# Interleaving the 128-column blocks of the up, down, output and gate weight tiles

## The chip, the core and the metric

The kernel runs on one core of a Trainium2 chip. The core has five engines with queues of their own: TensorE (PE in the rows, with its weight loads listed apart as PEld), VectorE (DVE), ScalarE (ACT), GpSimd (POOL) and SyncE (SP), which here issues the DMAs. The metric is the device time of one execution in microseconds (us), the median of several runs. The rows come from one profiled execution.

## What is computed

Two layers of a hybrid transformer block on 512 tokens with 1024 features, in float32. Cut to the lines whose weights the change touches (`w_out`, `w_ffn_up`, `w_ffn_down`, `w_ple_gate`):

```
merged = jnp.einsum('bsnd,nbsd->bsd', gates, branch)
x = x + rms_norm(merged @ w_out, g_post_mix)

h2 = rms_norm(x, g_pre_ffn)
f = jnp.square(jax.nn.relu(h2 @ w_ffn_up)) @ w_ffn_down
x = x + rms_norm(f, g_post_ffn)

ple = (p_i.astype(x.dtype) @ w_ple) * jax.nn.sigmoid(x @ w_ple_gate)
return x + rms_norm(ple, g_post_ple)
```

Ahead of these lines each layer has a wide input projection, a sparse attention, a linear recurrence, a spatial gate and a branch projection; their weights stay as they are.

## The kernel before

Activations lie transposed: features on the 128 partitions, the 512 tokens along the free dimension, so that a product of 1024 features is eight blocks of 128. A weight tile is a matrix of 128 partitions by 1024 floats, and for the four matrices of the change it holds the eight 128x128 blocks that make one output tile of 128 features: block k stands at columns 128k to 128k+127.

Weights come through one pipeline, in the order of the list `order`. `prep` (L230 and after) lets SyncE fetch a tile into `wr` (L236), rounds it on ScalarE into `wh` (L242), and lets VectorE subtract for the remainder `wl` (L243). `getw` hands the pair out and prepares up to three tiles ahead; four pairs of buffers turn.

A product in near-float32 precision is three matmuls in fp32r per block: `wh` with the high part of the activations, `wl` with the high part, `wh` with the low part (`mm3`, L296 to L299). The weight block is the stationary operand (128 columns, loaded by an LDWEIGHTS ahead of each matmul, the PEld rows), the activations are the moving one. `gemm` (L301) runs the eight blocks one after the other, so that a tile is 24 weight loads and 24 matmuls.

Which way a tile takes decides how many tokens move per load:

- `gemm` with all 512 tokens: all 32 down tiles of a layer, 28 of its 32 up tiles, five of eight output tiles, one of eight gate tiles.
- `gemm_halves` (L324 and after): the last three output tiles and the last three gate tiles, first for tokens 0 to 255, then for 256 to 511, so that the norm of the first half starts while the second is multiplied. A tile is then 48 loads and 48 matmuls of 256 tokens. It calls `gemm`, so its rows too bear L297 to L299.
- `gemm_arriving` (L337 and after, matmul at L355): several output tiles at once, block by block as the normed activations arrive. The first four up tiles go this way in halves of 256 tokens, the first four gate tiles with 512.

The input projection (95 of 303 tiles), the branches and the token-wise projections use the same pipeline and the same matmul helpers. The order in which the instructions stand on each engine is written by the program; a running count of estimated time (`tick`) places deferred tasks of the attention, and it doesn't look at the weights' layout.

`_pack` lays the weights out on the host, outside the measured time. In `tiles` the block index k is the slower column index.

Of the kernel before, what the change touches and what calls it, by code (L numbers as in the profile page):

```python
# [19 lines left out]
KT = 8  # L20
# [15 lines left out]
    + [f"g{n}_{d}" for n in range(3) for d in range(8)]  # L36
)
TILE_AT = {n: i for i, n in enumerate(TILES)}


V_PRE, V_POST, V_FFN, V_PFFN, V_PPLE = 0, 8, 16, 24, 32
# [9 lines left out]
def hybrid_block_kernel(ctx, tc, xT, pT, pos, vec, bsp, freq, w_in, w_tok, w_lru, w_sp, w_br, w_out, w_up, w_dn, w_ple, w_gate, out, depth=DEPTH, dbg=None):  # L51
    nc = tc.nc
    V, A, G, PE = nc.vector, nc.scalar, nc.gpsimd, nc.tensor
# [9 lines left out]
    def nm(p):  # L63
        uid[0] += 1
        return f"{p}_{uid[0]}"
# [7 lines left out]
    def bank():  # L73
        return pp.tile([128, 512], F32, tag="ps", name=nm("ps"), bufs=8)
# [8 lines left out]
    def width(r):  # L83
        return r.stop - r.start
# [82 lines left out]
    for l in range(depth):  # L167
        def t_in(n, l=l):
            order.append((("in", l, n), w_in[l, TILE_AT[n]]))

# [55 lines left out]
    prepared = {}  # L226
    LA = NWB - 1
# [18 lines left out]
    def getw(key, ahead=LA):  # L246
        assert order[nget[0]][0] == key, (order[nget[0]][0], key)
        nget[0] += 1
        while nprep[0] < min(nget[0] + ahead, len(order)):
            prep()  # L250
        return prepared.pop(key)

# [30 lines left out]
    def tick(us):  # L285
        clk[0] += us
        run_later()
        run_tasks()
# [4 lines left out]
            tick(0.3)  # L293


    def mm3(ps, wh, wl, xh, xl, start, stop):  # L296
        PE.matmul(ps, wh, xh, start=start, stop=False)  # L297
        PE.matmul(ps, wl, xh, start=False, stop=False)  # L298
        PE.matmul(ps, wh, xl, start=False, stop=stop)  # L299

    def gemm(ps, w, xs, kk, c0=0, st=None, r=FULL):  # L301

        h3, l3 = [v.rearrange("p (k c) -> p k c", k=kk) for v in w]
        for k in range(kk):
            if st is not None and k == kk - 2:
                st.partial()
            mm3(ps, h3[:, k, c0:c0 + 128], l3[:, k, c0:c0 + 128], xs[k][0][:, r], xs[k][1][:, r], k == 0, k == kk - 1)
            tick(0.65 * width(r) / S)

    @contextmanager  # L310
# [23 lines left out]
    def gemm_arriving(keys, xs, source, ranges, arrived=None, lag=LAG, tail=TAIL):  # L334


        n = len(keys)  # L337
        ws = [getw(key, 0) for key in keys[:-1]]
        pss = [bank() for _ in keys]
        last = {}  # L340
        for r in ranges:
            gen = source(r)
            for k in range(KT):
                with ordered(last):
                    next(gen)
                    todo = [(o, k) for o in range(len(ws))]
                    if len(ws) < n and k == lag:
                        ws.append(getw(keys[-1], 0))
                        todo += [(n - 1, q) for q in range(k + 1)]
                    if r is ranges[-1] and k >= KT - tail:  # L350
                        todo = [] if k < KT - 1 else [(o, q) for o in range(n) for q in range(KT - tail, KT)]
                    for i, (o, q) in enumerate(todo):
                        h3, l3 = [v.rearrange("p (k c) -> p k c", k=KT) for v in ws[o]]
                        for m in range(3):
                            PE.matmul(pss[o][:, r], (h3, l3, h3)[m][:, q], xs[q][m // 2][:, r], start=q == 0 and m == 0, stop=q == KT - 1 and m == 2)  # L355
                        if r is ranges[-1] and q == KT - 1 and o < n - 1:
                            prep()
                tick(0.65 * len(todo) * width(r) / S)
            if arrived is not None:
                arrived(r)  # L360
        while nprep[0] < nget[0] + LA:
            prep()
        return pss
# [84 lines left out]
    class Norm:  # L448
# [16 lines left out]
        def source(self, r):  # L465
            while r.start not in self.gens:
                tick(0.1)
            return self.gens[r.start]
# [41 lines left out]
    for key, src in order[:3]:  # L510
        raw = wp.tile([128, 1024], F32, tag="wr", name=nm("wr"), bufs=3)
        hi = wp.tile([128, 1024], F32R, tag="wh", name=nm("wh"), bufs=NWB)
        lo = wp.tile([128, 1024], F32R, tag="wl", name=nm("wl"), bufs=NWB)
# [3 lines left out]
    for k in range(KT):  # L517
        if k in FIRST:
            c = slice(128 * k, 128 * (FIRST + [KT])[FIRST.index(k) + 1])
# [12 lines left out]
    for l in range(depth):  # L532
# [45 lines left out]
        def tokens(n, fn):  # L578


            ws = [[v.rearrange("p (k c) -> p k c", k=2) for v in getw(("tok", l, n, c), LA if c == 0 else 0)] for c in range(4)]
            for t0 in (0, 2):
                pss = [bank(), bank()]
                for k in range(KT):
                    wh, wl = [v[:, k % 2] for v in ws[k // 2]]
                    for t, ps in enumerate(pss, t0):
                        xh, xl = [v[:, t * 128:(t + 1) * 128] for v in XS[k]]
                        for i, (x, w) in enumerate(((xh, wh), (xl, wh), (xh, wl))):
                            PE.matmul(ps, x, w, start=k == 0 and i == 0, stop=k == KT - 1 and i == 2)  # L589
                        tick(0.65)  # L590
                    if t0 == 2 and k in (1, 3, 5):
                        prep()
                for t, ps in enumerate(pss, t0):
                    fn(t, ps)
# [7 lines left out]
        for j in range(4):  # L602
            ps = first[j]
# [13 lines left out]
        ps = proj("ki")  # L617
# [28 lines left out]
        for j in range(4):  # L646
            ps = proj(f"qi{j}")
# [103 lines left out]
        for j in range(4):  # L751
            ps = proj(f"zu{j}")
# [1 line left out]
            V.tensor_mul(zz, ps, R)  # L754
            A.activation(gzu[:, j], zz, AF.Gelu_apprx_tanh)
        run_later(force=True)
        wsh, wsl = [w.rearrange("p (j c) -> p j c", j=4) for w in getw(("sp", l))]
        GG = []

        def gelu_gate(j, ahead=LA):  # L760
# [8 lines left out]
        for j in range(4):  # L769
# [3 lines left out]
            for hf in range(2):  # L773
                ps = bank()
# [4 lines left out]
                for s in range(2):  # L779
                    r = slice(64 * s, 64 * s + 64)  # L780
# [50 lines left out]

        for j in range(2, 4):
            gelu_gate(j)
        w3 = [w.rearrange("p (k c) -> p k c", k=8) for w in getw(("lru", l))]
        Rg = []
        for j in range(4):
            if j == 2:
# [6 lines left out]
            r, i = tmp(), tmp()  # L844
# [165 lines left out]
        for j in range(4):  # L1010
            f = rope(proj(f"q{j}"))
            q2, ql = (slot(f"A{j}", F32R), slot(f"A{4 + j}", F32R)), tmp(F32R)
            for s in range(2):
                r, other = slice(64 * s, 64 * s + 64), slice(64 - 64 * s, 128 - 64 * s)
# [15 lines left out]
        for d in range(8):  # L1030
            if d % 2 == 0:
                w = getw(("br", l, 0, d // 2))
            branch(0, d, w, YA, TH[d])
            hi, lo = mh[d // 4][:, d % 4], ml[d // 4][:, d % 4]
# [12 lines left out]
        for d in range(5):  # L1047
            ps = bank()
# [8 lines left out]
        ps = bank()  # L1057
# [52 lines left out]
        for c in range(2):  # L1110
            w = getw(("ple", l, c), ahead=1)
            if c == 1:
                bc = st3.rstd_bc()
            for i in range(4):
                ps = bank()
# [14 lines left out]
        for d in range(5):  # L1130
            if d < 4:
                ps = first[d]
            else:
                ps = bank()
# [29 lines left out]
def _pack(inputs):  # L1164
    import numpy as np

    def c(a):
        return np.ascontiguousarray(a)

    n = {k: np.asarray(v) for k, v in inputs.items()}  # L1170
    L = DEPTH
    r = {}
    r["xT"] = c(n["x"][0].T).reshape(8, 128, S)
    r["pT"] = c(n["p"][:, 0].transpose(0, 2, 1).reshape(L, 2, 128, S).transpose(0, 2, 1, 3))
    r["pos"] = c(n["positions"].reshape(4, 128).T)

    def cols(a):
        return a.reshape(L, -1, 128).transpose(0, 2, 1)

    r["vec"] = c(np.concatenate(  # L1180
        [cols(n[k]) for k in ("g_pre_mix", "g_post_mix", "g_pre_ffn", "g_post_ffn", "g_post_ple", "conv_w", "conv_b", "b_rg_a", "b_rg_x", "lru_lambda", "g_gmlp_v")],
        axis=2))
    r["bsp"] = c(n["b_spatial"].reshape(L, 4, 2, 128).transpose(0, 2, 1, 3).reshape(L, 2, 512))
    r["freq"] = _freq()

    def tiles(w, nk):

        m = w.shape[2] // 128
        return c(w.reshape(L, nk, 128, m, 128).transpose(0, 3, 2, 1, 4).reshape(L, m, 128, nk * 128))

    w = n["w_in"]
    q, k, v, qi, ki, wi, rest = np.split(w, np.cumsum([512, 512, 512, 512, 64, 8]).tolist(), axis=2)
    pad = np.zeros((L, D, 56), w.dtype)
    xr_zu, zv, g = np.split(rest, [1536, 2048], axis=2)
    r["w_in"] = tiles(np.concatenate([ki, wi, pad, qi, q, k, xr_zu, g], axis=2), 8)
    r["w_tok"] = c(np.stack([v, zv], 1).reshape(L, 2, 4, 2, 128, 512).transpose(0, 1, 2, 4, 3, 5).reshape(L, 2, 4, 128, 1024))
    lru = np.zeros((L, 128, 8, 128), w.dtype)
    for i, key in enumerate(("w_rg_a", "w_rg_x")):
        for b in range(8):
            o = 64 * (b % 2)  # L1200
            lru[:, o:o + 64, 4 * i + b // 2, o:o + 64] = n[key][:, b]
    r["w_lru"] = lru.reshape(L, 128, 1024)
    r["w_sp"] = c(n["w_spatial"].transpose(0, 3, 1, 2).reshape(L, 128, 1024))
    r["w_br"] = c(n["w_branch"].reshape(L, 3, 4, 128, 4, 256).transpose(0, 1, 4, 3, 2, 5).reshape(L, 3, 4, 128, 1024))
    r["w_out"] = tiles(n["w_out"], 8)
    r["w_up"] = tiles(n["w_ffn_up"], 8)
    r["w_dn"] = c(n["w_ffn_down"].reshape(L, 4, 8, 128, 8, 128).transpose(0, 1, 4, 3, 2, 5).reshape(L, 4, 8, 128, 1024))
    r["w_ple"] = c(n["w_ple"].reshape(L, 2, 128, 2, 512).transpose(0, 3, 2, 1, 4).reshape(L, 2, 128, 1024))
    r["w_gate"] = tiles(n["w_ple_gate"], 8)
    return r  # L1210


# [17 lines left out]
```

## Time and profile before

| | us |
|---|---|
| median of 3 runs (lowest, highest) | 1858.88 (1858.13, 1859.21) |
| profiled execution, whole | 1859.11 |
| its span, first to last instruction | 1857.4 |
| TensorE matmul busy | 1804.0 (97%) |
| TensorE weight load busy | 1507.9 (81%) |
| VectorE busy | 1161.0 (63%) |
| ScalarE busy | 800.9 (43%) |
| GpSimd busy | 361.3 (19%) |

TensorE has 8798 matmuls and as many weight loads in the record. A matmul's busy time in a row includes the time in which its last columns travel through the array, and so rows of successive matmuls overlap; what one costs in a stream is the distance between two starts. The same holds for the loads: a row's duration is longer than what a load takes from the next one. PEclk, the clock that TensorE was granted, is 1.00 (2.4 GHz) in nearly the whole span, and 0.50 (1.2 GHz) in a few short stretches.

### The profile page before, as it was taken

How to read it: one execution, taken by the hardware profiler on the slowest of the kernel's cores; microseconds unless marked ns; L12 is line 12 of the kernel's file. 1: busy time of each engine (PE TensorE's matmuls, PEld its weight loads, DVE VectorE, ACT ScalarE, POOL GpSimd, SP SyncE). 2: the span in 40 equal slices, each digit the busy share in tenths (PEclk: the TensorE clock that was granted, in tenths of full speed). 3: DMA queues.
4: the chain of work that ended last, by engine and by line, in shares of the span. 5: the costliest groups of instructions: out<-in, count | busy, mean ns of one | idle time of the engine just before them, and what ended most of it. 6: DMA issues, size and time to landing. Idle time of an engine off the chain costs nothing.

```text
span 1857.4 us, 22874 instructions
## 1 busy us (share of the span) xinstructions
PE 1804.0 (97%) x8798; PEld 1507.9 (81%) x8798; DVE 1161.0 (63%) x1939; ACT 800.9 (43%) x1292; POOL 361.3 (19%) x292
## 2 busy tenths in 40 slices
PE   8899999999999999999998999999999999999997
PEld 7787777888888888888887877877888888888886
DVE  6689986666386253533685999866563852545355
ACT  5466435564353231323554572455544432222233
POOL 3513212210140000003354141222003200000033
PEclk9999999999999999999999999999999999999998
DMA  5122222222223222232212122221222222222321
GB/s 172 63 91 90 87 97 84 76 78 82 80 91 103 100 93 102 91 114 91 89 60 97 66 93 92 102 80 69 91 80 91 91 91 102 92 101 94 111 80 58
DMA packets 49678, 167.77 MB, mean 90 GB/s; under 512 B 6048, under 2 KB 8864, under 8 KB 49568
## 3 DMA queue, kind: packets, MB, share of 16 engines
q1 hardware_dynamic: 47376, 163.64, 25.7%
q10 hardware_dynamic: 2192, 2.67, 0.4%
q8 instruction: 69, 1.13, 0.2%
q14 instruction: 41, 0.34, 0.1%
HBM read 164.19 MB, written 2.10 MB: 90 GB/s over the span
## 4 chain that ended last, share of the span: by engine, by line
PE 72%; DVE 14%; POOL 5%; issue 4%; ACT 4%; DMA 0%; SPq 0%; POOLq 0%; DVEq 0%; ACTq 0%
PE ps L297 20%; PE ps L299 20%; PE ps L298 20%; PE ps L589 4%; PE ps L355 4%; DVE wl L243 2%; DVE tmp L706 2%; DVE m L704 2%; POOL tmp L574 1%; POOL tmp L575 1%; PE ps L958 1%; POOL sacc L397 1%; POOL X L482 1%; PE ps L671 1%; DVE tmp L781 1%
## 5 line engine op out<-in xcount | busy, mean ns | idle before, releaser
L242 ACT CAST wh<-wr 128x1024 fp32r<-128x1024 f32 x303 | 316.7, 1049 | 453.2 <-PE ps L299 369.2
L243 DVE TENSOR_TENSOR wl<-wr,wh 128x1024 fp32r<-128x1024 f32 x303 | 386.0, 1278 | 190.7 <-ACT wh L242 189.9
L297 PE MATMUL ps<-xh,wh 128*128 128x512 f32 (+1 forms) x1296 | 502.2, 388 | 0.0
L298 PE MATMUL ps<-xh,wl 128*128 128x512 f32 (+1 forms) x1296 | 495.1, 382 | 3.0 <-DVE wl L243 3.0
L299 PE MATMUL ps<-xl,wh 128*128 128x512 f32 (+1 forms) x1296 | 495.4, 382 | 0.0
L397 POOL TENSOR_TENSOR sacc<-sacc,tmp 128x256 f32<-128x256 f32 (+1 forms) x99 | 109.7, 1109 | 893.7 <-issue 584.5
L299 PEld LDWEIGHTS ps<-xl,wh 128*128 128x128 f32 x1296 | 243.7, 188 | 48.2
L298 PEld LDWEIGHTS ps<-xh,wl 128*128 128x128 f32 x1296 | 244.0, 188 | 46.9 <-DVE wl L243 3.8
L297 PEld LDWEIGHTS ps<-xh,wh 128*128 128x128 f32 x1296 | 243.8, 188 | 45.5 <-issue 1.9
L299 PE MATMUL ps<-V,wh 128*128 128x512 f32 (+1 forms) x528 | 195.5, 370 | 0.0
L297 PE MATMUL ps<-K,wh 128*128 128x512 f32 (+1 forms) x432 | 158.2, 366 | 0.0
L298 PE MATMUL ps<-K,wl 128*128 128x512 f32 (+1 forms) x432 | 157.9, 365 | 0.0
L299 PE MATMUL ps<-B,wh 128*128 128x512 f32 x336 | 131.0, 390 | 0.0
L297 PE MATMUL ps<-A,wh 128*128 128x512 f32 x320 | 125.0, 391 | 0.0
L298 PE MATMUL ps<-A,wl 128*128 128x512 f32 x320 | 124.6, 389 | 0.0
L1089 DVE TENSOR_TENSOR M<-M,ps 128x512 f32<-128x512 f32 x48 | 33.0, 688 | 141.4 <-PE ps L299 141.4
L299 PEld LDWEIGHTS ps<-V,wh 128*128 128x128 f32 x528 | 99.5, 188 | 16.8
L1077 DVE TENSOR_TENSOR tmp<-ps,R 128x512 f32<-128x512 f32 x64 | 43.9, 691 | 108.4 <-PE ps L299 108.4
L355 PE MATMUL ps<-xl,wh 128*128 128x256 f32 (+1 forms) x264 | 88.2, 334 | 7.7 <-DVE xl L502 6.9
L297 PEld LDWEIGHTS ps<-K,wh 128*128 128x128 f32 x432 | 81.5, 189 | 13.2
L298 PEld LDWEIGHTS ps<-K,wl 128*128 128x128 f32 x432 | 81.5, 189 | 13.1
L355 PE MATMUL ps<-xh,wh 128*128 128x256 f32 (+1 forms) x264 | 86.5, 328 | 1.0 <-ACT xh L492 1.0
(237 smaller groups left out, 2738.5 us busy)
## 6 DMA issues: line engine op xcount, KB each, us to landing
wr<-in_w_in_dram SPq DMA_DIRECT2D x95, 512.0 KB, 3.2
wr<-in_w_up_dram SPq DMA_DIRECT2D x64, 512.0 KB, 3.2
wr<-in_w_dn_dram SPq DMA_DIRECT2D x64, 512.0 KB, 3.2
wr<-in_w_br_dram SPq DMA_DIRECT2D x24, 512.0 KB, 3.2
wr<-in_w_tok_dram SPq DMA_DIRECT2D x16, 512.0 KB, 3.2
wr<-in_w_out_dram SPq DMA_DIRECT2D x16, 512.0 KB, 3.2
wr<-in_w_gate_dram SPq DMA_DIRECT2D x16, 512.0 KB, 3.2
X<-in_xT_dram SPq DMA_DIRECT2D x8, 256.0 KB, 5.2
```

The costliest lines, as they stand in the source:

```text
L242: A.copy(hi, raw)
L243: V.tensor_sub(lo, raw, f32v(hi))
L297: PE.matmul(ps, wh, xh, start=start, stop=False)
L298: PE.matmul(ps, wl, xh, start=False, stop=False)
L299: PE.matmul(ps, wh, xl, start=False, stop=stop)
L355: PE.matmul(pss[o][:, r], (h3, l3, h3)[m][:, q], xs[q][m // 2][:, r], start=q == 0 and m == 0, stop=q == KT - 1 and m == 2)
L397: G.tensor_add(sacc[:, r], sacc[:, r], self.q[r.start, r.stop])
L589: PE.matmul(ps, x, w, start=k == 0 and i == 0, stop=k == KT - 1 and i == 2)
L704: V.max(m8, (sc if r == 0 else wk)[:, :n])
L706: V.match_replace(wk[:, :n], m8, (sc if r == 0 else wk)[:, :n], -3.0e38)
L1077: V.tensor_mul(t, ps, R)
L1089: V.tensor_add(F[d], F[d], ps)
```

## The change

The eight blocks of a tile are laid into each other column by column. With a step of n, n neighbouring blocks form a group, and column c of the group's blocks stand side by side: column c of block k lies at position (k // n) * 128n + c * n + k % n of the tile. The step is 8 for the down and output tiles, 4 for the up tiles and 2 for the gate tiles. A stationary block is then read as 128 floats at a distance of 8, 4 or 2 floats (32, 16 or 8 bytes) where they were neighbours. `_pack` does the laying out; `getw` returns a third value, a function that gives the view of block k; the callers that need the plain pair take the first two. On every engine the same instructions stand in the same order with the same waits; the DMAs, ScalarE's rounding and VectorE's subtraction work on whole tiles as before. Only the access pattern of the stationary operand differs.

```
+STEP = {"up": 4, "dn": 8, "gate": 2, "out": 8}
...
-        return prepared.pop(key)
+        hi, lo = prepared.pop(key)
+        return hi, lo, lambda kk: blocks(key, (hi, lo), kk)
...
+    def blocks(key, w, kk):
+
+
+        n = STEP.get(key[0])
+        if n is None:
+            b = [v.rearrange("p (k c) -> p k c", k=kk) for v in w]
+            return lambda m, k, c0=0: b[m][:, k, c0:c0 + 128]
+        b = [v.rearrange("p (a c b) -> p a b c", b=n, c=128) for v in w]
+        return lambda m, k, c0=0: b[m][:, k // n, k % n]
...
-        h3, l3 = [v.rearrange("p (k c) -> p k c", k=kk) for v in w]
+        b = w[2](kk)
...
-            mm3(ps, h3[:, k, c0:c0 + 128], l3[:, k, c0:c0 + 128], xs[k][0][:, r], xs[k][1][:, r], k == 0, k == kk - 1)
+            mm3(ps, b(0, k, c0), b(1, k, c0), xs[k][0][:, r], xs[k][1][:, r], k == 0, k == kk - 1)
...
+    def mixed(key, a):
+
+        return c(a.reshape(a.shape[:-1] + (8 // STEP[key], STEP[key], 128)).swapaxes(-2, -1).reshape(a.shape))
...
-    r["w_out"] = tiles(n["w_out"], 8)
-    r["w_up"] = tiles(n["w_ffn_up"], 8)
+    r["w_out"] = mixed("out", tiles(n["w_out"], 8))
+    r["w_up"] = mixed("up", tiles(n["w_ffn_up"], 8))
...
-    r["w_gate"] = tiles(n["w_ple_gate"], 8)
+    r["w_gate"] = mixed("gate", tiles(n["w_ple_gate"], 8))
```

`gemm_arriving` takes its blocks from the same function, and `w_dn` is wrapped in `mixed("dn", ...)` in the same way.

## Rows read from the trace of the kernel before

**Rows 1.** The page's first part: busy us (share of the span) and instructions.

```profile
PE 1804.0 (97%) x8798; PEld 1507.9 (81%) x8798; DVE 1161.0 (63%) x1939; ACT 800.9 (43%) x1292; POOL 361.3 (19%) x292
```

**Rows 2.** Busy time by stretch: up and down products of layers 0 and 1.

```profile
core 0: us, PE busy (x) PEld busy (x) DVE busy (x) ACT busy (x) POOL busy (x), PEclk, DMA share, GB/s
546.80:866.30 319.50, 319.50 (x1413) 264.63 (x1412) 149.37 (x180) 90.81 (x108) 10.42 (x6) 1.00 0.29 99
1463.70:1783.10 319.40, 319.40 (x1411) 264.51 (x1410) 149.28 (x179) 90.81 (x108) 10.43 (x6) 1.00 0.29 99
```

**Rows 3.** Timeline, a down product: start us, duration us, engine, line, operation.

```profile
699.68 0.39 PE L299 MATMUL ps<-B,wh 128*128 128x512 f32 x1
...
701.04 0.39 PE L299 MATMUL ps<-B,wh 128*128 128x512 f32 x1
...
699.91 0.19 PEld L298 LDWEIGHTS ps<-A,wl 128*128 128x128 f32 x1
700.14 0.19 PEld L299 LDWEIGHTS ps<-B,wh 128*128 128x128 f32 x1
```

**Rows 4.** Timeline, loads with two moving columns each (sums for the norm).

```profile
866.51 0.63 PEld L407 LDWEIGHTS ps<-ones,sacc 128*128 128x128 f32 x5
```

**Rows 5.** Timeline, output tiles in halves of 256 tokens.

```profile
496.73 0.28 PE L297 MATMUL ps<-K,wh 128*128 128x256 f32 x1
...
498.53 0.28 PE L297 MATMUL ps<-K,wh 128*128 128x256 f32 x1
```

**Rows 6.** Busy time by stretch: output halves, the first up tiles, both layers.

```profile
495.30:513.10 17.80, 17.80 (x151) 17.80 (x150) 4.77 (x7) 8.44 (x17) 6.49 (x8) 1.00 0.21 74
513.20:540.60 27.40, 25.80 (x206) 24.65 (x205) 22.76 (x45) 16.53 (x37) 19.31 (x23) 1.00 0.12 39
1430.00:1457.40 27.40, 25.81 (x205) 24.68 (x205) 22.75 (x45) 16.46 (x37) 19.34 (x23) 1.00 0.12 40
```

**Rows 7.** Waits of TensorE from 495.3 to 546 us: total, times, longest.

```profile
PE ps L355 <- DVE xl L502: 1.0, 2, 0.7
PE ps L433 <- POOL rt L427: 0.4, 1, 0.4
```

**Rows 8.** Timelines and their granted clock (PEclk): 256 and 512 tokens at 0.50.

```profile
931.80:934.00 2.20, 2.20 (x12) 2.20 (x12) 1.92 (x6) 1.24 (x4) 2.18 (x3) 0.50 0.16 65
...
932.00 0.41 PE L355 MATMUL ps<-xh,wl 128*128 128x256 f32 x1
...
933.28 0.41 PE L355 MATMUL ps<-xh,wl 128*128 128x256 f32 x1
...
1000.28 0.63 PE L589 MATMUL ps<-wh,xl 128*128 128x512 f32 x1
...
1001.99 0.63 PE L589 MATMUL ps<-wl,xh 128*128 128x512 f32 x1
```

**Rows 9.** Timeline and granted clock of the warm-up: bf16, 64 moving columns.

```profile
6.20:7.00 0.80, 0.80 (x34) 0.80 (x31) 0.49 (x1) 0.80 (x3) 0.00 (x0) 1.00 1.14 100
...
6.12 0.92 PEld L113 LDWEIGHTS <-bias 128*128 128x128 bf16 x29
```

More of the change, by code (lines that the diff above doesn't have):

```diff
@@ L352, in gemm_arriving @@
                     for i, (o, q) in enumerate(todo):
-                        h3, l3 = [v.rearrange("p (k c) -> p k c", k=KT) for v in ws[o]]
+                        b = ws[o][2](KT)
                         for m in range(3):
-                            PE.matmul(pss[o][:, r], (h3, l3, h3)[m][:, q], xs[q][m // 2][:, r], start=q == 0 and m == 0, stop=q == KT - 1 and m == 2)
+                            PE.matmul(pss[o][:, r], b((0, 1, 0)[m], q), xs[q][m // 2][:, r], start=q == 0 and m == 0, stop=q == KT - 1 and m == 2)
                         if r is ranges[-1] and q == KT - 1 and o < n - 1:
@@ L578, in tokens @@
         def tokens(n, fn):
-            ws = [[v.rearrange("p (k c) -> p k c", k=2) for v in getw(("tok", l, n, c), LA if c == 0 else 0)] for c in range(4)]
+            ws = [[v.rearrange("p (k c) -> p k c", k=2) for v in getw(("tok", l, n, c), LA if c == 0 else 0)[:2]] for c in range(4)]
             for t0 in (0, 2):
@@ L756, in hybrid_block_kernel @@
         run_later(force=True)
-        wsh, wsl = [w.rearrange("p (j c) -> p j c", j=4) for w in getw(("sp", l))]
+        wsh, wsl = [w.rearrange("p (j c) -> p j c", j=4) for w in getw(("sp", l))[:2]]
         GG = []
@@ L833, in hybrid_block_kernel @@
             gelu_gate(j)
-        w3 = [w.rearrange("p (k c) -> p k c", k=8) for w in getw(("lru", l))]
+        w3 = [w.rearrange("p (k c) -> p k c", k=8) for w in getw(("lru", l))[:2]]
         Rg = []
@@ L1204, in _pack @@
     r["w_br"] = c(n["w_branch"].reshape(L, 3, 4, 128, 4, 256).transpose(0, 1, 4, 3, 2, 5).reshape(L, 3, 4, 128, 1024))
-    r["w_out"] = tiles(n["w_out"], 8)
-    r["w_up"] = tiles(n["w_ffn_up"], 8)
-    r["w_dn"] = c(n["w_ffn_down"].reshape(L, 4, 8, 128, 8, 128).transpose(0, 1, 4, 3, 2, 5).reshape(L, 4, 8, 128, 1024))
+    r["w_out"] = mixed("out", tiles(n["w_out"], 8))
+    r["w_up"] = mixed("up", tiles(n["w_ffn_up"], 8))
+    r["w_dn"] = mixed("dn", c(n["w_ffn_down"].reshape(L, 4, 8, 128, 8, 128).transpose(0, 1, 4, 3, 2, 5).reshape(L, 4, 8, 128, 1024)))
     r["w_ple"] = c(n["w_ple"].reshape(L, 2, 128, 2, 512).transpose(0, 3, 2, 1, 4).reshape(L, 2, 128, 1024))
-    r["w_gate"] = tiles(n["w_ple_gate"], 8)
+    r["w_gate"] = mixed("gate", tiles(n["w_ple_gate"], 8))
     return r
```

## The prediction

> **What bounds the kernel now.** I read the shares first: matmuls are busy in 97% of the span, weight loads in 81%, no other engine in more than 63% [rows 1]. Then I looked at the largest stretch that the change touches, the up and down products: in 319.5 us of each layer TensorE has no idle time at the full clock, while VectorE is busy for 149 us and ScalarE for 91 [rows 2]. So these stages cost what the stream of loads and matmuls on TensorE costs, and nothing that another engine gains or loses is seen.
>
> Next, the distance between starts. In the timeline of a down product six matmuls of 512 tokens take 701.04 - 699.68 = 1.36 us, 0.227 each [rows 3]. The load of each following matmul starts as its predecessor starts, so the two run side by side, and the question is how much of the 0.227 a load needs. Its duration of 0.19 us contains latency. The products with `ones` show it better: there only two columns move per load, and five loads lie within 0.63 us, the last with the 0.19 of the loads in [rows 3]: (0.63 - 0.19) / 4 = 0.110 us from load to load [rows 4]; with times rounded to 0.01 us that is 0.108 to 0.113, and I use 0.111. Beside a matmul of 512 tokens a load thus has 0.227 - 0.111 = 0.116 us to spare: it could double and still just fit (0.222 against 0.227).
>
> With 256 tokens it is another matter. In the output halves 15 matmuls take 498.53 - 496.73 = 1.80 us, 0.120 each [rows 5], against a load of 0.111: the load has 0.009 to spare, and a slower one is on the path at once.
>
> **The change part by part.** It moves, adds and removes no instruction. DMAs, rounding and subtraction treat the whole tile, and the extra views are made while the program is built: these edits cost nothing, with no cover needed. What is left is 128 stationary columns read at a distance of 8, 4 or 2 floats. The affected matmuls, both layers together:
>
> - 512 tokens, step 8 or 4: down 64 tiles x 24 = 1536; up 56 x 24 = 1344; output 10 x 24 = 240. Together 3120.
> - 256 tokens, step 8 or 4: output 6 x 48 = 288; the first four up tiles 8 x 48 = 384. Together 672.
> - Step 2: gate, 240 of 512 tokens and 288 of 256.
>
> No row of this kernel shows a load at a distance. The lower bound is a load that doesn't change (x1), and a load that disturbs the stream less lies below nothing; that is a rival. For the upper bound I take the only loads here that are read in another way, the bf16 loads of the warm-up: 29 loads of 128 columns in 0.92 us, at most 0.032 each at the same clock [rows 9], against 0.111. The same number of columns can thus differ by 3.5 according to how they are read, and I let a load at a distance cost up to four times as much (0.444). Between x1 and x4 no row is nearer to one end; I take their middle in ratio, x2 = 0.222 us, for the steps 4 and 8, and x1 for the step 2, which still finds every second float of what it passes.
>
> The Trainium skill, page "SBUF — State Buffer", section "Specifications (TRN2)", speaks against the change: a line has 16 bytes, and two hits per line are needed for full bandwidth. By it the step 2 (two floats to a line) is free, and 4 and 8 (one to a line) pay alike. It gives no size, and no run so far shows it; the split between steps above would be the same by it, and steps priced evenly would add the gate's 288 short matmuls, 29 us.
>
> The terms, with loads of 0.222:
>
> 1. *512 tokens.* 0.222 still fits into 0.227, so the least is 0. But load and stream side by side do cost something at the full clock: at half clock 256 tokens take (933.28 - 932.00) / 6 = 0.213 [rows 8], half of which is 0.107; load 0.111 and stream 0.107 together take 0.120 [rows 5], 0.009 over the longer. So 0 to 0.009 per matmul. At half clock, where both are slower, 0.213 is just what 256 columns take at 1.2 GHz, nothing added, which speaks for 0. I take the middle, 0.004: 3120 x 0.004 = 12.5 us (0 to 28).
> 2. *Output halves.* From 0.120 to 0.222: 288 x 0.102 = 29.4 us. Nothing covers it, since TensorE is busy throughout the stretch [rows 6].
> 3. *First up tiles.* A stretch of 27.4 us for 192 matmuls per layer [rows 6]. The matmuls take 192 x 0.120 = 23.0, norm sums and turns about 1.3 (eight loads of 0.111 and four like them), and 3.1 are idle or paced by arriving activations; TensorE's named waits are 1.0 for `xl` and 0.4 for the norm's factor [rows 7]. With 0.222 the matmuls take 42.6 and arrivals no longer pace them, but the named waits remain: 42.6 + 1.3 + 1.4 = 45.3. That is 17.9 us more per layer, 35.8 for both (33 to 39).
> 4. *Gate.* Step 2 at x1: 0.
>
> Sum: 12.5 + 29.4 + 35.8 + 0 = 77.7 us. Later VectorE and ScalarE have more time, so nothing else becomes late: beside slower matmuls their work is hidden as before. The profiled execution took 1859.11 us, 0.2 above the median of 1858.88, so 77.7 over either gives **1937 us**, 4.2% slower. With loads of 1.5 times (0.167) the halves alone cost 672 x 0.047 = 32 us; with a little more than x2, where the 512-token term reaches 0.013 each, the sum is 41 + 65 + some 7. The case's own range is 1890 to 1975.
>
> **The rivals.**
>
> *The load keeps its pace.* If one float per read is all that a load ever takes, a distance costs nothing: 1859 us. For it: at half clock the load slows with the array (TensorE's 256-token distance doubles to 0.213 and no load sticks out [rows 8]), so the array, not the reading, may set the 0.111. Against it: the bf16 loads are 3.5 times as fast [rows 9].
>
> *Loads at a distance disturb the stream, or take four times as long.* At full clock a matmul of 512 tokens takes 0.227, while half of the half-clock distance, (1001.99 - 1000.28) / 4 / 2, is 0.214 [rows 8]; with 256 tokens it is 0.120 against 0.107. Both exceed by 0.013, whatever the length, so this is a price per load and matmul pair. If it is the load's reading that holds up the moving operand's, and four places have to be read where one was, it is 0.053: 0.040 more for 3792 matmuls and 0.013 for the gate's 528 make 152 + 7 = 159 us, and up to 195 with the doubled load on the halves: 2018 to 2053. With loads of 0.444 the 512-token matmuls are bound by them too: 3120 x 0.217 + 672 x 0.324 = 895 us, some 2750. It decides as soon as a load exceeds 0.227. The Trainium skill, same page, section "Who interferes with whom", speaks against the first form: TensorE's moving operand and its weight load have independent read ports. No row tells whose the 0.013 is.
>
> *Reading at a distance disturbs less* (ends on the other side). If the 0.013 comes from neighbouring floats of the load meeting the stream's reading in the same place, spreading them may remove it: at most 3120 x 0.0135 = 42 us, 1817; half of it 1838. For it: the excess is there only at full clock. Against it: it is equal for all moving tensors in [rows 3, 5], which lie at different places.
>
> **How the numbers follow.** Load about twice as long, 43%: 1890 to 1975, likeliest 1937. Pace kept, 24%: 1859. Stream disturbed 12% (2018 to 2053) or four times as long 6% (some 2750). Disturbs less, 15%: 1817 to 1855. The range 1836 to 2040 leaves out the four-fold case, the top of the disturbed one and the lower half of the faster one, some 17 in 100 together. A measurement of this kernel can tell 0.2% (3.7 us) from no change. Faster 0.15, within 0.2% 0.24, slower 0.61.
>
> **What would show it.** In the profile after: the distance of the 256-token starts in the output halves (0.222, or 0.120 if the pace is kept) and of the first up tiles; the distance in a down product (0.227 to 0.236); the weight loads' mean duration, 0.30 at steps 4 and 8 against 0.19 at the gate and the input projection, which is not touched. The forecast is wrong if steps 4 and 8 differ, if step 2 pays, or if the down products lengthen by more than the halves do.

## The result and the profile after

The changed kernel took 1976.5 us (median of four runs, 1973.7 to 1977.1), the kernel before 1858.5 on the same chip: a ratio of 1.0632, 95% interval 1.0614 to 1.0651. The change costs 118 us. The forecast was 1937, in a range of 1836 to 2040: right in direction and mechanism, 40 us short in size, and 1.5 us beyond the 1975 at which the forecast's own case ended. The profiled execution after took 1976.1 us, of which the span is 1974.4, against 1857.4 for the span before.

The first part of the page after, to be laid beside [rows 1]:

```profile
PE 1923.6 (97%) x8798; PEld 1751.0 (89%) x8798; DVE 1159.6 (59%) x1939; ACT 801.3 (41%) x1292; POOL 362.9 (18%) x292
```

The same instructions ran. Weight loads are busy 243 us longer, matmuls 120 us, and every other engine as long as before; so the new time is on TensorE alone. Its time without work hardly changed: 53.4 us of the span before (1857.4 - 1804.0), 50.8 after.

Next the stretches. The columns are those of [rows 2]; the rows are most of the up and down products of layer 0 (1392 matmuls), one block of eight up tiles (192 matmuls), one of eight down tiles (192), the output halves with what stands beside them, the first up tiles, and a piece of the gate with 512 tokens.

```profile
core 0: us, PE busy (x) PEld busy (x) DVE busy (x) ACT busy (x) POOL busy (x), PEclk, DMA share, GB/s
585.00:918.50 333.50, 333.50 (x1392) 333.42 (x1392) 147.38 (x177) 88.94 (x106) 8.63 (x5) 1.00 0.29 94
694.50:739.60 45.10, 45.10 (x193) 45.10 (x193) 23.15 (x29) 13.24 (x16) 0.00 (x0) 1.00 0.29 94
739.70:786.50 46.80, 46.80 (x193) 46.80 (x193) 16.51 (x18) 9.03 (x9) 0.00 (x0) 1.00 0.27 90
497.40:532.70 35.30, 35.30 (x152) 35.30 (x151) 7.28 (x12) 9.05 (x18) 7.31 (x8) 1.00 0.15 48
532.80:578.70 45.90, 45.90 (x205) 45.90 (x204) 20.84 (x40) 16.50 (x36) 18.48 (x22) 1.00 0.09 26
939.00:961.30 22.30, 22.30 (x97) 18.47 (x96) 16.01 (x20) 11.25 (x18) 5.68 (x5) 1.00 0.16 53
```

In the first row the loads are busy in all 333.5 us, where before they had gaps (264.63 of 319.50 in [rows 2]). That fits stages that now wait for their loads, but load rows overlap one another (the output halves were full of them before, 17.80 of 17.80 us in [rows 6]), so it does not prove it. Per matmul an up tile (step 4) costs 45.1 / 192 = 0.235 us, a down tile (step 8) 46.8 / 192 = 0.244, a gate tile (step 2) 22.3 / 96 = 0.232, where all of them stood at 0.227 before [rows 3]. The first up tiles went from 27.4 [rows 6] to 45.9 us, and the 1.4 us of named waits there [rows 7] are gone: TensorE is busy throughout.

The timeline of the output halves (start us, duration us, engine, line, operation), to be laid beside [rows 5]; between the two rows lie six more starts:

```profile
499.80 0.41 PE L312 MATMUL ps<-K,wl 128*128 128x256 f32 x1
...
501.48 0.40 PE L313 MATMUL ps<-V,wh 128*128 128x256 f32 x1
```

1.68 us for seven distances is 0.240, where it was 0.120. The weight loads of five stretches, grouped (busy us, mean ns of one | idle before them): up tiles, down tiles, output halves, gate with 512 tokens, gate halves:

```profile
L311 PEld LDWEIGHTS ps<-xh,wh 128*128 128x128 f32 x64 | 19.8, 310 | 0.0
...
L313 PEld LDWEIGHTS ps<-B,wh 128*128 128x128 f32 x64 | 21.1, 329 | 0.0
...
L313 PEld LDWEIGHTS ps<-V,wh 128*128 128x128 f32 x20 | 6.8, 338 | 0.0
...
L369 PEld LDWEIGHTS ps<-xh,wl 128*128 128x128 f32 x32 | 6.2, 193 | 1.3
...
L313 PEld LDWEIGHTS ps<-xl,wh 128*128 128x128 f32 x28 | 5.5, 195 | 0.0
```

At steps 4 and 8 a load lasts 0.31 to 0.34 us, at step 2 0.19, as all did before. These durations are 0.08 to 0.1 us longer than the distance from load to load (before: 0.19 against the 0.111 of [rows 4]), so they alone do not give the pace of the loads; the experiments do.

**Where the 118 us lie.** The distance between starts, averaged over all matmuls of a kind in both layers, before and after, times their number:

| matmuls | step | before us | after us | number | difference us |
|---|---|---|---|---|---|
| down, 512 tokens | 8 | 0.2268 | 0.2445 | 1536 | 27.2 |
| up, 512 tokens | 4 | 0.2271 | 0.2358 | 1344 | 11.7 |
| output, 512 tokens | 8 | 0.2267 | 0.2446 | 240 | 4.3 |
| gate, 512 tokens | 2 | 0.2267 | 0.2333 | 240 | 1.6 |
| output halves | 8 | 0.1209 | 0.2412 | 288 | 34.6 |
| first up tiles (stretches of 27.4 and 45.9 us) | 4 | | | 2 x 192 | 37.0 |
| gate halves | 2 | 0.1209 | 0.1212 | 288 | 0.1 |

Together 116.5, which is all but 1.5 us of the difference. The tiles of the input projection, which were not touched, kept their mean of 0.233.

### The profile page after: what moved, and what is told of

It reads as the page before. It is cut to its first block, busy times and chain, and to the rows that moved or that the text cites. A ratio compares the mean times of both kernels' runs of the same rounds, so it can differ in the third digit from the quotient of the medians.

```text
span 1974.4 us, 22874 instructions
## 1 busy us (share of the span) xinstructions
PE 1923.6 (97%) x8798; PEld 1751.0 (89%) x8798; DVE 1159.6 (59%) x1939; ACT 801.3 (41%) x1292; POOL 362.9 (18%) x292
## 4 chain that ended last, share of the span: by engine, by line
PE 74%; DVE 14%; POOL 4%; issue 4%; ACT 3%; DMA 0%; SPq 0%; POOLq 0%; DVEq 0%; ACTq 0%
PE ps L311 20%; PE ps L312 20%; PE ps L313 20%; PE ps L369 7%; PE ps L603 3%; DVE wl L246 2%; DVE tmp L720 2%; DVE m L718 2%; POOL tmp L588 1%; POOL tmp L589 1%; PE ps L972 1%; PE ps L685 1%; DVE tmp L795 1%; DVE M L624 1%; PE ps L958 1%
## 5 line engine op out<-in xcount | busy, mean ns | idle before, releaser
L313 PEld LDWEIGHTS ps<-xl,wh 128*128 128x128 f32 x1296 | 298.6, 230 | 30.6
L312 PEld LDWEIGHTS ps<-xh,wl 128*128 128x128 f32 x1296 | 299.1, 231 | 29.7 <-DVE wl L246 3.8
L311 PEld LDWEIGHTS ps<-xh,wh 128*128 128x128 f32 x1296 | 298.8, 231 | 28.4 <-issue 1.9
L313 PE MATMUL ps<-V,wh 128*128 128x512 f32 (+1 forms) x528 | 213.1, 404 | 0.0
L312 PE MATMUL ps<-K,wl 128*128 128x512 f32 (+1 forms) x432 | 176.0, 407 | 0.0
L311 PE MATMUL ps<-K,wh 128*128 128x512 f32 (+1 forms) x432 | 175.4, 406 | 0.0
L313 PEld LDWEIGHTS ps<-V,wh 128*128 128x128 f32 x528 | 161.2, 305 | 3.7
L312 PEld LDWEIGHTS ps<-K,wl 128*128 128x128 f32 x432 | 142.8, 330 | 0.0
L311 PEld LDWEIGHTS ps<-K,wh 128*128 128x128 f32 x432 | 142.3, 329 | 0.1
L369 PE MATMUL ps<-xh,wh 128*128 128x256 f32 (+1 forms) x264 | 101.3, 384 | 1.3 <-ACT xh L506 1.3
```

The costliest lines, as they stand in the source:

```text
L369: PE.matmul(pss[o][:, r], b((0, 1, 0)[m], q), xs[q][m // 2][:, r], start=q == 0 and m == 0, stop=q == KT - 1 and m == 2)
```

## The experiments

The edits are cut to the lines that matter (where `_pack` follows the same change, it is left out), and in the kernels of plain streams the letters stand for the numbers that each stream has.

The leading theory after the result: a matmul starts as late as the longer of two things allows, its stream of moving columns and its load, and a load at a distance of 4 or more floats takes 0.23 to 0.24 us instead of 0.111. Rivals: a load that disturbs the stream, and the rule of lines. For this rule, the Trainium skill, page "SBUF — State Buffer", section "Specifications (TRN2)", gives lines of 16 bytes and wants two hits on each for full bandwidth, so that step 2 would be free and steps 4 and 8 alike.

**Streams of plain matmuls.** A kernel of nothing but matmuls, 32 for each step and each number of moving columns, one source line per stream:

```diff
+o = j % n if n > 1 else 128 * (j % 8)
+PE.matmul(ps[:, 0:N], w[:, o:o + n * 127 + 1:n], x[:, 0:N], start=True, stop=True)
```

> Leaves out the whole block: only streams of matmuls, 32 to a line, each with a weight load of 128 columns, at 64, 128, 256, 384 and 512 moving columns and at load steps of 1, 2, 3, 4, 5, 6, 8 and 16 floats; then loads of 32 and 64 columns, and bf16 loads at steps 1 to 16. Theory A (a load has a duration set by its step, and the distance of matmul starts is the longer of load and stream): step 1 and 2 about 0.111 us at 64 to 256 columns and 0.227 at 512; steps 4 and up about 0.233 to 0.245 at every number of columns, 64 as well as 512. Theory B (reading at a distance holds up the moving operand): the distance grows with the columns at every step, at step 8 by about 0.018 over step 1 at each length, so about 0.13 at 256 columns. The line rule: step 3 (12 bytes) lies between steps 2 and 4, bf16 loads stay fast up to step 4 (8 bytes) and slow down from step 8 (16 bytes).

Each row gives a line's matmuls: shortest, median and longest duration in ns, then the first and the last start in us; (last - first) / 31 is the distance, good to 0.003 us, since these starts are rounded to 0.1. The distances in the text are means of the unrounded ones. The lines: 256 columns at steps 2, 3, 4, 8 and 16 (L59, L60, L61, L64, L65), 384 at step 4 (L69), 512 at steps 1, 2, 3, 4, 8 and 16 (L74 to L77, L80, L81), 128 at step 4 at the half clock (L53), and bf16 with 64 columns at steps 4 and 8 (L87, L88).

```profile
L59 PE MATMUL ps<-x,w x32: 278/283/285, 132.3 to 136.1; 128*128 128x256 f32 x32
L60 PE MATMUL ps<-x,w x32: 328/339/346, 136.2 to 141.6; 128*128 128x256 f32 x32
L61 PE MATMUL ps<-x,w x32: 394/396/397, 141.8 to 149.0; 128*128 128x256 f32 x32
L64 PE MATMUL ps<-x,w x32: 396/404/410, 163.8 to 171.3; 128*128 128x256 f32 x32
L65 PE MATMUL ps<-x,w x32: 381/386/393, 171.6 to 178.5; 128*128 128x256 f32 x32
L69 PE MATMUL ps<-x,w x32: 391/394/401, 195.5 to 202.7; 128*128 128x384 f32 x32
L74 PE MATMUL ps<-x,w x32: 389/389/397, 232.7 to 239.7; 128*128 128x512 f32 x32
L75 PE MATMUL ps<-x,w x32: 394/394/397, 240.0 to 247.2; 128*128 128x512 f32 x32
L76 PE MATMUL ps<-x,w x32: 393/397/401, 247.4 to 254.7; 128*128 128x512 f32 x32
L77 PE MATMUL ps<-x,w x32: 394/398/401, 255.0 to 262.3; 128*128 128x512 f32 x32
L80 PE MATMUL ps<-x,w x32: 401/410/418, 277.7 to 285.3; 128*128 128x512 f32 x32
L81 PE MATMUL ps<-x,w x32: 393/398/405, 285.5 to 292.9; 128*128 128x512 f32 x32
L53 PE MATMUL ps<-x,w x32: 416/435/435, 90.0 to 97.3; 128*128 128x128 f32 x32
L87 PE MATMUL ps<-y,v x32: 196/198/199, 309.7 to 310.8; 128*128 128x64 bf16 x32
L88 PE MATMUL ps<-y,v x32: 224/227/229, 310.8 to 312.7; 128*128 128x64 bf16 x32
```

The granted clock of the two stretches in which the lines lie (columns here: PE, PEld, ACT and POOL busy, PEclk, DMA share, GB/s):

```profile
25.20:130.00 104.80, 104.80 (x471) 104.80 (x471) 0.00 (x0) 0.00 (x0) 0.50 0.00 0
131.00:352.00 221.00, 218.26 (x1129) 193.07 (x1131) 0.58 (x1) 0.00 (x0) 1.00 0.01 3
```

With 256 columns the distances are 0.120 at step 2, 0.175 at 3, 0.233 at 4, 0.241 at 8 and 0.223 at 16. At step 4 it is 0.233 whether 128, 256 or 384 columns move, and at half clock as at full: there the load alone sets it, and it does not go with TensorE's clock, while at step 1 it does (0.112 at full, 0.213 at half). So with 256 columns the kernel's numbers are those of its loads.

With 512 columns: 0.2276 at step 1, 0.2333 at 2, 0.2354 at 3, 0.235 at 4, 0.2455 at 8, 0.2365 at 16. At step 8 the load (0.241) is longer than the stream's 0.227, and the distance follows it, with 4 ns more. At step 4 the load's length is not needed for the 0.235: steps 3 and 16, whose loads take 0.175 and 0.223 and would be hidden, cost as much beside 512 columns. What they pay is more than the longer of load and stream.

The Trainium skill's rule of lines, from the page and section named above, has its boundary in the right place: bf16 doubles from 0.033 to 0.062 at a step of 16 bytes, as fp32 does. But the size is neither even beyond it (0.233, 0.241, 0.223), nor nothing ahead of it: 12 bytes cost 0.175, and step 2 costs 6 ns beside 512 columns.

**The short matmuls with plain blocks.** The changed kernel, with step 1 again for output tiles 5 to 7 and the first four up tiles:

```diff
-n = STEP.get(key[0])
+n = None if key[0] == "out" and key[2] >= 5 or key[0] == "up" and key[2] == 0 and key[3] < 4 else STEP.get(key[0])
```

> The changed kernel, with plain blocks again in the tiles that are multiplied in halves of 256 tokens (output tiles 5 to 7 and the first four up tiles). Theory A with costs that stay where they arise: the 672 short matmuls return from 0.233 to 0.241 us to 0.120, which gives back 35 us in the output halves and 37 in the first up tiles: 1976.5 - 72 = 1905 us. Rival (slower halves also delay the norm, so that arrivals come late, or the cost is all in the long products): 1890 or less in the first case, above 1950 in the second.

Measured 1904.99 us, ratio to before 1.0252 (1.0234 to 1.0271): 71.5 us of the 118 are gone, the two terms of short matmuls in the table (71.6). The four runs spread over 5.7 us, so that so close an agreement is in part chance. The halves' timeline, seven starts between the two rows, is back at 0.119:

```profile
498.41 0.28 PE L312 MATMUL ps<-K,wl 128*128 128x256 f32 x1
...
499.36 0.28 PE L311 MATMUL ps<-K,wh 128*128 128x256 f32 x1
```

**Down alone.** Step 8 for the down weights, all others plain:

```diff
-STEP = {"up": 4, "dn": 8, "gate": 2, "out": 8}
+STEP = {"dn": 8}
```

> The kernel before with step 8 for the down tiles alone. If the distance of 0.2445 us of their 1536 matmuls against 0.2267 is all: 1858.5 + 27 = 1886 us. If the long products were hidden behind their loads as the forecast had it (0.227 to 0.231): 1859 to 1865. If a load at step 8 cost four times as much: 2190.

Measured 1886.69 us, 28.2 above before; ratio 1.0155 (1.0140 to 1.0170). In its timeline the plain up tiles keep 0.227 (nine distances in the first pair of rows), the down tiles take 0.246 (five in the second):

```profile
600.11 0.39 PE L313 MATMUL ps<-xl,wh 128*128 128x512 f32 x1
...
602.15 0.39 PE L313 MATMUL ps<-xl,wh 128*128 128x512 f32 x1
...
649.93 0.41 PE L311 MATMUL ps<-K,wh 128*128 128x512 f32 x1
...
651.16 0.40 PE L313 MATMUL ps<-V,wh 128*128 128x512 f32 x1
```

So each matmul pays for its own load, and nothing is passed on to its neighbours.

**All steps 2.**

```diff
-STEP = {"up": 4, "dn": 8, "gate": 2, "out": 8}
+STEP = {"up": 2, "dn": 2, "gate": 2, "out": 2}
```

> Step 2 for all four matrices. By the line rule (two floats to a line) and by theory A (load of 0.111 hidden under 0.227) the time of the kernel before: 1858 to 1860 us. By theory B, read from the gate's matmuls of 512 tokens in the changed kernel (0.2333 against 0.2267 at step 2, and 0.120 unchanged with 256): 3360 x 0.0066 = 22 us more, 1881.

Measured 1880.96 us, ratio 1.0121 (1.0104 to 1.0138): the value that a price of 6.6 ns for every 512-token matmul gives, not that of a free step. The up and down stretch of [rows 2], by window, and two starts of output halves, eleven distances apart:

```profile
546.80:866.30 319.50, 319.50 (x1372) 264.28 (x1371) 146.71 (x176) 87.39 (x104) 6.92 (x4) 1.00 0.30 97
...
497.72 0.28 PE L312 MATMUL ps<-K,wl 128*128 128x256 f32 x1
...
499.04 0.28 PE L311 MATMUL ps<-K,wh 128*128 128x256 f32 x1
```

1372 instead of 1413 matmuls fit into the 319.5 us, 0.2329 each instead of 0.2261; with 256 tokens it is 0.120, as before. This is not a load that has outgrown its cover: alone it takes 0.118 at step 2 (seen with 64 columns at full clock in the first kernel of streams), half of the 0.233, and its row lasts 264.28 / 1371 = 0.193 us, 5 ns more than before. The longer of load and stream is thus not the whole story: something of 6 to 7 ns at step 2 shows beside 512 columns only.

**All steps 4.**

```diff
-STEP = {"up": 4, "dn": 8, "gate": 2, "out": 8}
+STEP = {"up": 4, "dn": 4, "gate": 4, "out": 4}
```

> Step 4 for all four matrices. From the distances seen at step 4 (0.2358 us with 512 tokens, 0.2333 with 256): 3360 long matmuls x 0.0091 = 31 us; halves of output and gate tiles 576 x 0.113 = 65 us; first up tiles 37 us; 1858.5 + 133 = 1991 us. If the price of a step rose with the distance (step 8 dearer than 4 because it skips more), step 4 would bring less for down and output, 16 us less than their step 8; if only the gate's step 2 were free because the gate's stage has cover, its 288 short matmuls would not lengthen and the time would be 1959.

Measured 1988.25 us, ratio 1.0693 (1.0675 to 1.0711). The gate's halves now stand 0.234 apart, as the output halves do (eleven distances in these rows), and the matmuls of the down tiles are closer than at step 8 (0.235 against 0.2445): that steps 4 and 8 differ belongs to the load, and not to the tile or its place in the program.

```profile
497.82 0.39 PE L311 MATMUL ps<-K,wh 128*128 128x256 f32 x1
...
500.39 0.39 PE L313 MATMUL ps<-V,wh 128*128 128x256 f32 x1
```

**Further steps, and the moving operand at a distance.** The kernel of plain streams with steps up to 32, and three streams with the moving columns spread instead:

```diff
+PE.matmul(ps, w[:, o:o + 128], v[:, j:j + 2 * 511 + 1:2], start=True, stop=True)
```

> Leaves out the whole block: streams of 32 matmuls a line again, at 512 and 256 columns, with load steps of 1, 2, 4, 7, 8, 9, 12, 16, 24 and 32 floats; then step 1 with moving columns read at steps 2, 4 and 8, and steps 1 and 8 with the same two weight blocks all the time. If every step from 4 up means one read per float, loads at 256 columns lie between 0.22 and 0.245 us at all of them, with no growth up to 32; if a load's price grows with the distance, 24 and 32 lie above 0.25. If the moving operand has the same threshold, 512 columns take about 0.227 at step 2 and 0.43 or more at steps 4 and 8.

256 columns at steps 4, 12 and 32 (L58, L62, L65), then plain loads with the moving operand at step 2 (L67, the row holds every second one of its 32, so 30 distances):

```profile
L58 PE MATMUL ps<-x,w x32: 393/400/401, 106.1 to 113.4; 128*128 128x256 f32 x32
L62 PE MATMUL ps<-x,w x32: 421/432/438, 136.6 to 144.9; 128*128 128x256 f32 x32
L65 PE MATMUL ps<-x,w x32: 376/388/399, 160.4 to 167.3; 128*128 128x256 f32 x32
L67 PE MATMUL ps<-w x16: 613/636/652, 167.6 to 181.2; 128*128 128x512 f32 x16
```

The price does not grow with the distance: 0.237, 0.234, 0.241, 0.240 at steps 4, 7, 8, 9, then 0.269 at 12, 0.222 at 16, 0.253 at 24, 0.225 at 32. Steps 16 and 32 are the cheapest beyond step 3, and 12 and 24 the dearest, above the 0.245 that was expected at most. What makes this pattern was not followed. The moving operand is the more sensitive of the two, and not at the step that was expected: at step 2 already the distance of 512 tokens doubles to 0.453, and stays near it at steps 4 and 8 (0.461, 0.431).

**Places.** In the streams before, step 1 had 0.227 in one kernel and 0.233 in another, whose tiles lay elsewhere. Hence a kernel of streams with 512 columns in which the start of the stationary block or that of the moving operand is shifted:

```diff
+PE.matmul(ps, w0[:, s:s + n * 127 + 1:n], x0[:, m:m + 512], start=True, stop=True)
```

> Leaves out the whole block: streams of 32 matmuls of 512 columns a line, one stationary and one moving tile, at load steps of 1, 2 and 4, with the stationary block beginning at 0 to 1024 floats into its tile, and then with the moving operand beginning at 0 to 512 floats into its own. The question is what the 0.0066 us are that step 2 costs beside 512 columns and not beside 256 or 384. If they belong to the step (more reading beside the stream): step 1 at 0.227 and step 2 at 0.233 at every place. If they belong to where load and stream meet: both steps lie between 0.226 and 0.237 and change with the place, with no fixed order between them. Step 4 in both cases 0.231 to 0.240, since its load alone takes 0.233.

Stationary block shifted by 16 columns (L47) and by 64 (L49), both at step 1, and step 2 unshifted (L57):

```profile
L47 PE MATMUL ps<-x,w x32: 392/395/398, 54.1 to 61.4; 128*128 128x512 f32 x32
L49 PE MATMUL ps<-x,w x32: 389/389/396, 69.0 to 76.1; 128*128 128x512 f32 x32
L57 PE MATMUL ps<-x,w x32: 394/394/394, 127.3 to 134.5; 128*128 128x512 f32 x32
```

At step 1 the distance is 0.227 to 0.228 when the shift is a multiple of 64 columns (256 bytes), and 0.231 to 0.2334 at all other shifts, whichever operand is shifted. At step 2 it is 0.230 to 0.2334 everywhere, at step 4 0.233 to 0.240. So 0.227 is the special case, and step 2 costs what a plain block costs that lies elsewhere.

**The kernel before with its weights 64 bytes further.** If that holds in the kernel, a place alone must make it slower, with no step at all:

```diff
+wp.tile([128, 16], F32, tag="shift", name="shift")
```

> The kernel before, step 1 everywhere, with one idle piece of 16 columns of fp32 (64 bytes) ahead of the weight tiles in SBUF, so that every weight tile lies 64 bytes further and nothing else moves. Place theory, from the streams of plain matmuls where 512-token ones stood 0.227 us apart when the stationary block's start was a multiple of 64 columns and 0.2334 when it was 16 columns off: some 6300 matmuls of 512 tokens by 0.0064 make about 40 us, 1899 us, with the 512-token starts at 0.2334 and the 256-token ones left at 0.121. If the distance depends on the step between columns alone, nothing moves: 1858.5 us and 0.227.

Measured 1884.01 us, ratio 1.0133 (1.0116 to 1.0150). It moved, by 25.5 us instead of 40. The stretch of [rows 2]:

```profile
546.80:866.30 319.50, 319.50 (x1372) 257.41 (x1371) 146.66 (x176) 87.72 (x105) 7.16 (x5) 1.00 0.30 98
```

It is the rate of the kernel with steps 2, while a load's row lasts 257.41 / 1371 = 0.188 us, as before the shift; so a longer load is not what costs the 6.6 ns here. The mean of all down matmuls is 0.2334, as expected. The expected sum was too large in three ways: the halves became a little shorter (0.1190 against 0.1209), the input projection's matmuls lost 4 ns each and not 6.6, and those of the branch product 3. TensorE's time without work fell from 53.4 to 44.2 us, so longer matmuls filled waits there. By the distances of all weight tiles the sum is 31 us; where the 5.6 between it and 25.5 went was not followed.

**Both shifted.** Last, whether a start has to lie well by itself, or the two against each other:

```diff
+for s, m in ((0, 0), (16, 16), (16, 80), (16, 0), (0, 16), (32, 32), (32, 0), (8, 8), (8, 0)):
+    PE.matmul(ps, w0[:, s:s + n * 127 + 1:n], x0[:, m:m + 512], start=True, stop=True)
```

> Streams of 32 plain matmuls each (step 1 between columns, 512 moving columns), nothing else on TensorE; the start of the stationary block and the start of the moving operand are shifted one by one and both together, by 1 to 32 columns off a multiple of 64. If what counts is where the two lie against each other, equal shifts (16 and 16, 32 and 32, 8 and 8, or 16 and 80) stand 0.227 us apart, as both unshifted do, and unequal ones 0.230 to 0.2334. If each start by itself has to be a multiple of 64 columns, equal shifts cost 0.230 to 0.2334 too. The same pairs at step 2 should stay at 0.230 to 0.2334 by either. With 256 moving columns (four more pairs) the shift should cost nothing or take 0.001 to 0.003 away, as in the kernel with shifted weights. The kernel computes nothing of the reference but these streams.

Step 1 with shifts of 16 and 16, 16 and 80, 16 and 0 (L43 to L45), then 256 columns with 16 and 16, and with 16 and 0 (L71, L72):

```profile
L43 PE MATMUL ps<-x,w x32: 387/389/397, 23.8 to 30.9; 128*128 128x512 f32 x32
L44 PE MATMUL ps<-x,w x32: 389/389/389, 31.1 to 38.1; 128*128 128x512 f32 x32
L45 PE MATMUL ps<-x,w x32: 394/394/397, 38.4 to 45.6; 128*128 128x512 f32 x32
...
L71 PE MATMUL ps<-x,w x32: 278/283/283, 228.0 to 231.7; 128*128 128x256 f32 x32
L72 PE MATMUL ps<-x,w x32: 276/276/286, 231.8 to 235.3; 128*128 128x256 f32 x32
```

Equal shifts of 8, 16, 24 and 32 columns, and 16 against 80, give 0.227 to 0.228; unequal ones 0.229 to 0.2334. (Equal shifts of 1 and 4 columns don't: 0.238 and 0.231.) So at shifts of at least 8 columns it is the place of the load against that of the stream that counts. With 256 columns it is the other way round: 0.120 with equal places, 0.1134 to 0.114 with unequal ones, close to the 0.112 of the load alone. At step 2 all 14 pairs stand at 0.230 to 0.2334. Why step 2 has no good place was not found out.

Plain blocks that lie unequal for the short matmuls and equal for the long ones might gain a little over the kernel before: by the streams at most 960 x 0.007 = 7 us, an estimate. In the shifted kernel, however, output and gate halves gained only 0.002 each, and no kernel with both placements was tried. No whole block that ran was faster than the one before.

## Why the prediction was right, and where its size was off

**What bounds the kernel.** Held. All of the 118 us stand on TensorE, no other engine's work changed, and the terms of the table add up with nothing given back elsewhere.

**The load's length.** This is the first of two steps that mis-sized the sum. The prediction took the middle in ratio of its bounds, 0.222 us, and said that a load decides for long matmuls as soon as it exceeds 0.227. It measured 0.233 at step 4 and 0.241 at step 8: only 5 and 9% more, but the 0.227 lies in between. At step 8 what the prediction held to be just covered was not. At step 4 the load is too long as well, but the streams do not show that this is what the up tiles pay for.

**Term 1, 512 tokens.** Forecast 12.5 us (0 to 28), measured 43.2. Three quarters of the missing 40 us are here (31). At step 8 (down and output, 31.5 us) the load alone exceeds 0.227 by 14 ns, which makes some 25 us; the forecast's sum had nothing for this. The second mis-sized step is the 0.004 for load and stream side by side, the middle between 0 and 0.009. The up tiles (11.7 us) pay 9 ns each, the upper end, and loads that would be hidden pay 6 to 10 beside 512 columns: 6.6 at step 2, 9 at step 3, 10 at step 16. How much of the up tiles' 9 ns is this price and how much the 6 ns by which a load of 0.233 exceeds 0.227 was not separated. The prediction had worked out the neighbouring case, "a little more than x2, where the 512-token term reaches 0.013 each", at 41 + 65 + 7 us, which is 113, close to what came (43.2 + 71.6). With the load's length unknown, that case deserved more weight: a term that is small on one side of 0.227 and grows by 3.1 us for each further ns is not at its mean when the length is at its middle.

**Term 2, output halves.** Forecast 29.4, measured 34.6: 288 x 0.120 instead of x 0.102, the load again (0.241 for 0.222). **Term 3, first up tiles.** Forecast 35.8 (33 to 39), measured 37.0. Here the longer load added some 2.5 us per layer (192 x 0.013) and the named waits of 1.4 us went away; the two partly cancel.

**Term 4, gate.** Forecast 0, measured 1.7, nearly all with 512 tokens. With 256 tokens the distance stays at 0.12. The 6.6 ns beside 512 are what a plain block costs that lies unequal to its stream; at step 2 no place was found below 0.230.

**The signs it named.** Of the three that were to prove it wrong, two came: steps 4 and 8 differ (0.233 and 0.241), and step 2 pays (0.2333 for 0.2267). The third did not: down products lengthened by 0.018, the halves by 0.120. The mechanism, a load that lasts about twice as long, stood; that steps 4 and 8 cost the same and that step 2 is free, which it had also taken, fell.

**The rivals.** *Pace kept* fell with the first stream. The clock argument for it was half right: at step 1 the load does go with TensorE's clock (0.112 and 0.213), but from step 4 on it doesn't (0.233 at both). *Four times as long* fell: no step gave more than 2.5 times 0.111 (0.269 at step 12). *Disturbed stream* fell at its price of 0.040 per matmul: with down alone spread, the neighbouring up tiles kept 0.227, and the down tiles took 0.245 where their load alone takes 0.241. A smaller disturbance, of 6 to 10 ns, does exist, and the rival that *spreading disturbs less* had its idea, that it matters where load and stream lie. But equal places, which the kernel before has by its 0.227 and 0.120, are the good case for 512 tokens, so that spreading could only lose there; unequal places gain 6 ns with 256 tokens, where the steps 4 and 8 lost 113 to 120. On this the Trainium skill, page "SBUF — State Buffer", section "Who interferes with whom", says that TensorE's two operands have independent read ports; the streams agree in the main (a load of 0.233 us beside 512 columns makes 0.235), yet a load with 0.116 us to spare still moved the distance by 6.6 ns when its place was shifted, so the two are not wholly independent here. What the two share was not found out.

## What to carry to other kernels

Keep the columns of a stationary block next to each other: read at a distance of 16 bytes or more, the load of 128 columns takes two to two and a half times as long, and every fp32r matmul then costs 0.22 to 0.27 us, with 128 moving columns as with 384; 512 columns, 0.227 us, did not hide it. When a hidden cost grows towards its cover, work out the sum on both sides of the point where it comes out, since at step 8 a load 9% longer than assumed, past that point, decided a fifth of this result. And when two versions of a kernel place their tiles differently, compare the distance between starts before blaming the code: 64 bytes of shift alone cost 1.3%.

## What the runs showed of the hardware

- A load's price by the distance of its columns is not even: 0.112 us at step 1, 0.118 at 2, 0.175 at 3, 0.233 at 4, 0.227 at 5, 0.229 at 6, 0.241 at 8, 0.269 at 12, 0.222 at 16, 0.253 at 24, 0.225 at 32 (fp32r, 128 columns, full clock; steps 1 and 2 with 64 moving columns, the others with 256).
- From step 4 on a load takes as long at half of TensorE's clock as at the full one (0.233 with 128 moving columns at a granted 0.50, 0.233 with 256 at 1.00); at step 1 it is 0.213 and 0.112. At half clock step 3 takes 0.213 too, where at the full one it takes 0.175 and step 1 0.112.
- Beside 512 moving columns a load that would be hidden still costs up to 10 ns: 0.227 at step 1 in an equal place, 0.233 at step 2, 0.2354 at 3, 0.2365 at 16, though these loads take 0.118, 0.175 and 0.223 alone. Beside 384 columns steps 1 and 2 both stand at 0.173.
- Fewer columns per load do not help a stream that is bound by its moving columns: plain loads of 32 and of 64 columns beside 512 moving ones gave 0.231 and 0.230.
- Spread moving columns cost more than spread stationary ones: already at step 2 the distance of 512-token matmuls doubles to 0.453.
- With load and stream in equal places 512 tokens take 0.227 and 256 take 0.120; in unequal places 0.229 to 0.2334 and 0.1134 to 0.114.
